# Conv's last three blocks by token half, conv's output products reordered, one query and key group normalized earlier, the first operand by single k tiles, and the last addition but one on GpSimd

## The chip, the cores and the metric

The kernel runs on one core of one Trainium2 chip. The metric is the device time of an execution in microseconds (us). Before the change the median of three executions is 1030.29 us (1028.41 to 1030.9). The engines go by their names in the profile: PE is TensorE (PEld its weight loads), DVE is VectorE, ACT is ScalarE, POOL is GpSimd, SP is SyncE, which issues most DMAs.

## The reference

Two decoder layers over 256 tokens of width 1024; the first mixes tokens by attention, the second by a convolution module. Each sublayer is normalized, scaled and shifted by vectors that come from a conditioning vector `c`, and gated.

```python
for i in range(2):
    mod = (silu(c) @ ada_w[i] + ada_b[i]).reshape(B, 3, 3, D)
    shift, scl, gate = mod[:, :, 0], mod[:, :, 1], mod[:, :, 2]
    pre = lambda z, j: rms_norm(z, norm_g[i, j]) * (1 + scl[:, j]) + shift[:, j]
    x = x + 0.5 * gate[:, 0] * swiglu_ffn(pre(x, 0), ffn_w_in[i, 0], ffn_w_out[i, 0])
    h = pre(x, 1)
    y = moba_attention(h, ...) if i == 0 else conformer_conv(h, ...)
    x = x + gate[:, 1] * y
    x = x + 0.5 * gate[:, 2] * swiglu_ffn(pre(x, 2), ffn_w_in[i, 1], ffn_w_out[i, 1])
# attention: 16 heads of 64, q and k RMS-normed per head, causal, ALiBi
# conv: u = h @ w_pw1 + b; u = a * sigmoid(g); 31-tap causal depthwise conv;
#       silu(layer_norm(u)) @ w_pw2 + b
```

## The kernel before

**Products.** Every large product is made in three: operand and weight are each split into a high part and a rest (`hh`, `hl` for the operand, `whi`, `wlo` for the weight), and PE adds hh·whi, hh·wlo and hl·whi (lines 675 to 677 in `mm3`). A weight tile of 128x1024 comes in by a DMA that SP issues (`raw`, L210); ACT makes `whi` (L250), DVE makes `wlo` (L225). Folds of the conditioning matrix run in between as chains of multiply-adds on DVE (L289, L291; L529, L531 for the first sublayer). All of this is one stream of steps: `take(n)` sets how many steps each following `block()` of products issues, so `take` and the place of the calls in the Python code set where the weight work stands in the queues of ACT and DVE. Six raw buffers and six split pairs go round.

**Order.** Nothing sorts the instructions: each engine runs its own in the order in which the code issues them, and an instruction that waits holds all behind it on its engine.

**Start.** The first operand is made by quarters `q` of the width (`early_turn`, L586 to L599). Per quarter ACT reads two k tiles from PSUM and scales them (L595, twice 128x256), copies both into `hh` in one instruction (L598, 128x512), and DVE subtracts for `hl` (L599, 128x512). Until the first product PE runs 8 idle matmuls (`IDLE_FIRST`).

**Attention.** The sublayer is an order written by hand, in which U(t, unit, u) is a block of projections, R(t, g) the sum of squares of one token half's query and key group (ACT L864, DVE L867 and L868 for `s`, and a power on POOL for `r`, L869), N(t, g) the multiplication by it (DVE L875, `z`), Q(t, g) its transposes on PE (L887) with copies on ACT, S scores (DVE L919 and ACT L925 behind them), M the division of the probabilities `p` (DVE L936), X their transposes (PE L943), V the products with the values. Its output operand is split at L966 and L967. R(1,1) comes a few calls ahead of N(1,1), with U(0,C,1) and V(0) between them.

**Convolution.** Eight blocks of 128 channels. U(b) projects a block, `glu` gates it (ACT L1096, DVE L1097), `park` and `spread` send it out and back by POOL's DMAs, `wide` makes a block's tap weights (POOL or DVE, L1050), C(b) is the depthwise convolution (64 matmuls, L1122, then ACT L1126 adds the bias into `v`), VT(b) transposes `v` to tokens by channels (PE L1136). When all eight blocks are there, `moments` and `norm` (DVE L1141 to L1152, POOL L1148) normalize a token half t, `swish(t, h)` transposes it back (PE L1159) with a Silu on ACT (L1163), `put(t, h)` makes `hh` and `hl` (DVE L1175, L1176), and O(t, j) is the output product, j over the four quarters of the contraction. `run_sums` is a group of 16 one-column matmuls (L347). `residual(t)` (DVE L609, L612) adds the result to `x`, then follows the next sublayer's normalization (POOL L631, DVE L638, PE L654, ACT and DVE L660 to L670); the callback `after()` is the one for token half 0. C(6) and C(7) run as two token halves of 128, C(0) to C(5) whole.

**End.** The last `residual` of each token half goes in pieces of 512, 256 and 256 columns; each piece is one multiplication (L609), one addition (L612), both on DVE, and one DMA to the output (L614).

## Time and profile before

| what | value |
|---|---|
| median of three executions | 1030.29 us |
| the profiled execution's own time | 1031.33 us |
| its span | 1029.6 us |
| PE busy in the span | 1013.7 us (98%) |
| DVE, ACT, POOL busy | 781.1, 488.9, 70.5 us |
| DMA moved | 256 MB, 249 GB/s |

The span is the stretch from the first instruction to the last that the profiler saw; 1.73 us of the execution's time lie around it. In order of time the span holds the first feed-forward sublayer (to about 213 us), attention (to about 340), two feed-forward sublayers (to about 722), the convolution (to about 836) and the last feed-forward sublayer. All times of instructions are us from the start of the span. "Busy" of PE counts an instruction as long as its results are on the way; matmuls overlap, and what counts for PE is the distance from one start to the next (about 0.23 us for a 128x512 product).

### The profile page before, as it was taken

Reading aid. Unit: us, or ns where it says so; the run is one execution under the profiler, and the core shown is the slowest. Engines: PE = TensorE matmul, PEld = TensorE weight load, DVE = VectorE, ACT = ScalarE, POOL = GpSimd, SP = SyncE. Lnnn points to the kernel's source line nnn. Section 1 sums busy time; section 2 is a strip of 40 time slices with the busy share of each in tenths; the row PEclk is TensorE's granted clock in tenths of the full one; section 3 lists DMA queues with packets and bytes.
Section 4 is the critical chain, followed back from the end, with each engine's and each line's share of the span. In section 5 each row is a group of like instructions: output and inputs, shape, how many; then the busy total and the mean of one; then the engine's idle time right before and its main releaser. Section 6 shows DMA issues by size and latency. Waiting matters only on the chain.

```text
span 1029.6 us, 14614 instructions
## 1 busy us (share of the span) xinstructions
PE 1013.7 (98%) x5457; PEld 821.8 (80%) x5457; DVE 781.1 (76%) x1167; ACT 488.9 (47%) x762; POOL 70.5 (7%) x123
## 2 busy tenths in 40 slices
PE   9999999999999999999999999999999999999998
PEld 6788787887776888887888887888986778888886
DVE  5789888989997788878778878786684788656633
ACT  4454344566675544444455444354522556444420
POOL 3000000002210000000010000000166000000000
PEclk9999999999999999999999999999999999999999
DMA  9989999948765399999839898886596468766611
GB/s 336 338 277 329 319 329 322 317 154 272 245 217 188 115 324 317 300 319 305 295 101 307 288 317 293 286 289 202 174 275 203 133 200 299 240 211 215 218 38 41
DMA packets 183754, 256.08 MB, mean 249 GB/s; under 512 B 9045, under 2 KB 132726, under 8 KB 183684
## 3 DMA queue, kind: packets, MB, share of 16 engines
q1 hardware_dynamic: 180928, 248.55, 72.4%
q0 software_dynamic: 2608, 6.55, 2.3%
q8 instruction: 43, 0.70, 0.3%
q14 instruction: 27, 0.22, 0.1%
q10 hardware_dynamic: 148, 0.06, 0.0%
HBM read 252.89 MB, written 2.23 MB: 248 GB/s over the span
## 4 chain that ended last, share of the span: by engine, by line
PE 82%; DVE 8%; ACT 4%; issue 3%; DMA 3%; POOL 0%; SPq 0%; POOLq 0%; DVEq 0%; ACTq 0%
PE u L677 15%; PE u L675 14%; PE u L676 14%; PE y L675 10%; PE y L677 10%; PE y L676 10%; DVE wlo L225 2%; DVE acc L291 2%; PE m L753 2%; PE m L1122 2%; ACT whi L250 1%; DMA raw<-in_conv_w_pw_dram 1%; ACT p L925 1%; DMA raw<-in_ffn_w_in_dram 1%; DMA raw<-in_attn_w_qkv_dram 1%
## 5 line engine op out<-in xcount | busy, mean ns | idle before, releaser
L225 DVE TENSOR_TENSOR wlo<-raw,whi 128x1024 fp32r<-128x1024 f32 x320 | 382.4, 1224 | 31.4 <-ACT whi L250 31.2
L250 ACT ACTIVATE whi<-raw 128x1024 fp32r<-128x1024 f32 x320 | 328.4, 1054 | 151.0 <-DMA raw<-in_ffn_w_in_dram 67.6
L675 PE MATMUL u<-whi,hh 128*128 128x512 f32 x672 | 266.4, 396 | 1.5 <-ACT hh L669 1.1
L677 PE MATMUL u<-whi,hl 128*128 128x512 f32 x672 | 262.9, 391 | 0.2
L676 PE MATMUL u<-wlo,hh 128*128 128x512 f32 x672 | 261.9, 390 | 0.3 <-DVE wlo L225 0.3
L291 DVE SCALAR_TENSOR_TENSOR acc<-raw,sc,acc 128x512 f32<-128x512 f32 x224 | 172.1, 768 | 5.0
L677 PEld LDWEIGHTS u<-whi,hl 128*128 128x128 f32 x672 | 126.1, 188 | 29.7 <-DVE hl L599 1.9
L675 PEld LDWEIGHTS u<-whi,hh 128*128 128x128 f32 x672 | 126.2, 188 | 28.1 <-ACT hh L669 1.9
L676 PEld LDWEIGHTS u<-wlo,hh 128*128 128x128 f32 x672 | 126.3, 188 | 25.6 <-DVE wlo L225 0.6
L675 PE MATMUL y<-whi,gh 128*128 128x512 f32 (+1 forms) x356 | 138.9, 390 | 0.2 <-ACT gh L761 0.2
L677 PE MATMUL y<-whi,gl 128*128 128x512 f32 (+1 forms) x356 | 137.9, 387 | 0.0
L676 PE MATMUL y<-wlo,gh 128*128 128x512 f32 (+1 forms) x356 | 137.8, 387 | 0.0
L675 PE MATMUL y<-whi,hh 128*128 128x512 f32 (+1 forms) x256 | 96.7, 378 | 1.5 <-DVE hh L1175 0.8
L762 DVE TENSOR_TENSOR gl<-m,gh 128x512 fp32r<-128x512 f32 (+1 forms) x48 | 31.0, 646 | 84.7 <-ACT gh L761 84.5
L677 PE MATMUL y<-whi,hl 128*128 128x512 f32 (+1 forms) x256 | 94.0, 367 | 0.0
L676 PE MATMUL y<-wlo,hh 128*128 128x512 f32 (+1 forms) x256 | 93.9, 367 | 0.0
L761 ACT ACTIVATE gh<-m 128x512 fp32r<-128x512 f32 (+1 forms) x48 | 27.0, 563 | 133.6 <-PE m L753 133.6
L723 ACT ACTIVATE sg<-u 128x256 f32<-128x256 f32 x84 | 32.1, 382 | 109.4 <-PE u L677 109.3
L675 PEld LDWEIGHTS y<-whi,gh 128*128 128x128 f32 x356 | 66.9, 188 | 15.5 <-issue 0.8
L677 PEld LDWEIGHTS y<-whi,gl 128*128 128x128 f32 x356 | 66.8, 188 | 14.3 <-DVE gl L762 0.4
L676 PEld LDWEIGHTS y<-wlo,gh 128*128 128x128 f32 x356 | 66.9, 188 | 13.3
L675 PEld LDWEIGHTS y<-whi,hh 128*128 128x128 f32 x256 | 48.7, 190 | 12.5 <-issue 3.5
(178 smaller groups left out, 872.7 us busy)
## 6 DMA issues: line engine op xcount, KB each, us to landing
raw<-in_ffn_w_in_dram SPq DMA_DIRECT2D x164, 512.0 KB, 5.0
raw<-in_ada_w_dram SPq DMA_DIRECT2D x144, 512.0 KB, 5.2
raw<-in_ffn_w_out_dram SPq DMA_DIRECT2D x88, 512.0 KB, 5.2
raw<-in_attn_w_qkv_dram SPq DMA_DIRECT2D x24, 512.0 KB, 5.0
raw<-in_conv_w_pw_dram SPq DMA_DIRECT2D x24, 512.0 KB, 6.3
raw<-in_ffn_w_in_dram SPq DMA_DIRECT2D x24, 256.0 KB, 4.5
R<-d POOLq DMA_DIRECT2D x32, 142.0 KB, 6.3
raw<-in_attn_w_o_dram SPq DMA_DIRECT2D x8, 512.0 KB, 4.5
```

Source lines behind the costliest of these rows:

```text
L225: (eng or nc.vector).tensor_tensor(lo, raw, hi.bitcast(F32), op=ALU.subtract)
L250: self.nc.scalar.activation(hi, self.like(self.raws[i], hi), AF.Copy)
L291: nc.vector.scalar_tensor_tensor(dst, raw[:, i, :], self.sc[:, k : k + 1], dst, op0=ALU.mult, op1=ALU.add)
L675: nc.tensor.matmul(out, lh, rh, start=start, stop=False)
L676: nc.tensor.matmul(out, lh, rl, start=False, stop=False)
L677: nc.tensor.matmul(out, ll, rh, start=False, stop=stop)
L723: nc.scalar.activation(sg, ps[:, 0:256], AF.Silu)
L753: nc.tensor.transpose(ps[:, o : o + P], g[:, t, k * P : k * P + P], self.ident)
L761: nc.scalar.activation(hi, src, AF.Copy)
L762: nc.vector.tensor_tensor(lo, src, hi.bitcast(F32), op=ALU.subtract)
L925: nc.scalar.activation(p[:, c0:c1], p[:, c0:c1], AF.Exp, bias=st[:, t : t + 1], scale=-1.0, accum_out=st[:, 2 + t : 3 + t],)
L1122: nc.tensor.matmul(ps[32 * g : 32 * g + 32, :], wd[b][:, q, g, :], R[b][:, g, 4 * q + t0 : 4 * q + t0 + n], start=q == 0, stop=q == 7,)
```

## The change

Line numbers of the changed kernel are 10 higher from `residual` on, 11 to 12 higher at the end of `conv`.

1. **First operand.** For the first quarter (q = 0) ACT copies each k tile into `hh` right behind its own scaling, and DVE subtracts each k tile by itself: two instructions of 128x256 for one of 128x512 on either engine. `IDLE_FIRST` goes from 8 to 6.
2. **Last residual.** The second and third piece share one `tmp` tile, and for token half 1 the addition of the second piece (columns 512 to 767) is issued to POOL.
3. **Attention.** N(1,1) moves ahead of U(0,C,1) and V(0).
4. **Convolution.** The five weight steps that the first block of the loop issued are spread as two in U(5) and two in U(6), with the rest later. C(5), C(6), C(7) run for token half 0 first, then for token half 1. swish(0, h) and put(0, h) stand between the second halves, `run_sums` behind them. The output products change from O(0,0) O(0,1) O(0,2) O(0,3) | residual(0) | O(1,0) O(1,1) after() O(1,2) O(1,3) to O(0,0) O(0,1) O(1,0) O(0,2) O(0,3) | residual(0) | O(1,1) O(1,2) after() O(1,3), and the takes around them change.

```diff
-IDLE_FIRST = 8
+IDLE_FIRST = 6
@@ early_turn, in the loop over the two k tiles i
-        nc.scalar.activation(hi, h, AF.Copy)
-        return lambda: nc.vector.tensor_tensor(lo, h, hi.bitcast(F32), op=ALU.subtract)
+            if not q:
+                nc.scalar.activation(hi[:, i, :], h[:, i, :], AF.Copy)
+        if q:
+            nc.scalar.activation(hi, h, AF.Copy)
+
+        def put():
+            for i in (slice(0, 1), slice(1, 2)) if not q else (slice(0, 2),):
+                nc.vector.tensor_tensor(lo[:, i, :], h[:, i, :], hi[:, i, :].bitcast(F32), op=ALU.subtract)
+
+        return put
@@ residual
-            tmp = self.two.tile([P, 512], F32, name="tmp", tag="tmp", bufs=1)[:, 0:n]
...
-            nc.vector.tensor_tensor(x[:, s], x[:, s], tmp, op=ALU.add)
+            c = slice(o % 512, o % 512 + n)
+            if c.start == 0:
+                half = self.two.tile([P, 512], F32, name="tmp", tag="tmp", bufs=1)
+            tmp = half[:, c]
+            nc.vector.scalar_tensor_tensor(tmp, y[h][:, c], f, gate[:, s], op0=ALU.mult, op1=ALU.mult)
+            eng = nc.gpsimd if t and o == 512 and last else nc.vector
+            eng.tensor_tensor(x[:, s], x[:, s], tmp, op=ALU.add)
@@ attention
-        U(0, C, 0), X(0), S(1), M(1), R(1, 1), Q(0, 1), U(0, C, 1), V(0), N(1, 1)
+        U(0, C, 0), X(0), S(1), M(1), R(1, 1), Q(0, 1), N(1, 1), U(0, C, 1), V(0)
@@ conv
         glu(4)
+        take(2)
         for b in range(4):
             if b < 3:
                 U(b + 5)
-            if b == 0:
+            if b == 1:
                 take(0)
...
-        C(5)
+        C(5, 0, P), VT(4), C(6, 0, P)
         self.step(), self.step()
-        VT(4), C(6, 0, P), VT(5), take(4), self.block(), C(7, 0, P), VT(6, (0,))
+        VT(5, (0,)), take(2), self.block(), C(7, 0, P), VT(6, (0,))
         take(0)
-        C(6, P, P), VT(7, (0,)), moments(0), norm(0, 0), norm(0, 1)
-        C(7, P, P), VT(6, (1,))
+        C(5, P, P), VT(7, (0,)), moments(0), norm(0, 0), norm(0, 1)
+        C(6, P, P), VT(5, (1,)), swish(0, 0)
+        C(7, P, P), VT(6, (1,)), put(0, 0), swish(0, 1)
+        VT(7, (1,)), moments(1), put(0, 1), norm(1, 0), norm(1, 1)
         self.run_sums(True)
-        VT(7, (1,)), swish(0, 0), moments(1), put(0, 0)
-        swish(0, 1), norm(1, 0), put(0, 1), norm(1, 1)
-        O(0, 0), swish(1, 0), O(0, 1), put(1, 0), swish(1, 1), put(1, 1), take()
-        O(0, 2), O(0, 3)
+        (the four y banks are allocated here)
+        O(0, 0), swish(1, 0), take(2), O(0, 1), put(1, 0), swish(1, 1), put(1, 1)
+        O(1, 0), O(0, 2), O(0, 3)
         self.residual(0, y[0], gate, 1.0)
-        O(1, 0), O(1, 1)
-        after()
-        O(1, 2), O(1, 3)
+        take(1), O(1, 1), O(1, 2), after(), take(0), O(1, 3)
         self.residual(1, y[1], gate, 1.0)
```

DVE in attention, around N(1,1), before the change (`s` is the sum of squares of R(1,1), `z` the product of N(1,1), `acc` a fold of the conditioning matrix, `wlo` a weight rest):

```order
L868 TENSOR_SCALAR s_2452<-s_2452 128x8
L291 SCALAR_TENSOR_TENSOR acc<-raw,sc,acc 128x512 x2
L225 TENSOR_TENSOR wlo<-raw,whi 128x1024
L875 TENSOR_TENSOR z<-y,r_2453 128x512
L225 TENSOR_TENSOR wlo<-raw,whi 128x1024
L291 SCALAR_TENSOR_TENSOR acc<-raw,sc,acc 128x512 x2
```

and with the change:

```order
L878 TENSOR_SCALAR s_2452<-s_2452 128x8
L885 TENSOR_TENSOR z<-y,r_2453 128x512
L291 SCALAR_TENSOR_TENSOR acc<-raw,sc,acc 128x512 x2
L225 TENSOR_TENSOR wlo<-raw,whi 128x1024 x2
L291 SCALAR_TENSOR_TENSOR acc<-raw,sc,acc 128x512 x2
```

Two folds and one weight rest that stood between `s` and `z` now stand behind `z`; `r`, which `z` reads, is made from `s` on POOL.

ACT in the convolution's loop, before the change (`whi` is a weight's high part, `sg` the sigmoid of a block, `v` a block's result with its bias):

```order
L250 ACTIVATE whi<-raw 128x8x128
L1096 ACTIVATE sg<-u,cols 128x256
L250 ACTIVATE whi<-raw 128x8x128 x3
L250 ACTIVATE whi<-raw 128x1024 x2
L1096 ACTIVATE sg<-u,cols 128x256
L1126 ACTIVATE v<-m,cols 128x256
```

and with the change:

```order
L250 ACTIVATE whi<-raw 128x8x128
L1106 ACTIVATE sg<-u,cols 128x256
L250 ACTIVATE whi<-raw 128x8x128 x2
L1106 ACTIVATE sg<-u,cols 128x256
L1136 ACTIVATE v<-m,cols 128x256
L250 ACTIVATE whi<-raw 128x8x128
L250 ACTIVATE whi<-raw 128x1024
L1106 ACTIVATE sg<-u,cols 128x256
```

The first `v`, and the `sg` ahead of it, stand behind two weights' high parts in place of five.

DVE at the end of the program, before the change (token half 1's last residual):

```order
L609 SCALAR_TENSOR_TENSOR tmp<-y,gate 128x512
L612 TENSOR_TENSOR x_118<-x_118,tmp 128x512
L609 SCALAR_TENSOR_TENSOR tmp<-y,gate 128x256
L612 TENSOR_TENSOR x_118<-x_118,tmp 128x256
L609 SCALAR_TENSOR_TENSOR tmp<-y,gate 128x256
L612 TENSOR_TENSOR x_118<-x_118,tmp 128x256
```

and with the change:

```order
L620 SCALAR_TENSOR_TENSOR tmp<-y,gate 128x512
L622 TENSOR_TENSOR x_118<-x_118,tmp 128x512
L620 SCALAR_TENSOR_TENSOR tmp<-y,gate 128x256 x2
L622 TENSOR_TENSOR x_118<-x_118,tmp 128x256
```

One of the two additions of 128x256 has left DVE; it is POOL's last instruction now, and SP's order of output DMAs is as it was.

## Rows read from the trace of the kernel before

**Rows 1.** The page's parts 1 and 4: busy per engine, the chain's shares.

```profile
PE 1013.7 (98%) x5457; PEld 821.8 (80%) x5457; DVE 781.1 (76%) x1167; ACT 488.9 (47%) x762; POOL 70.5 (7%) x123
PE 82%; DVE 8%; ACT 4%; issue 3%; DMA 3%; POOL 0%; SPq 0%; POOLq 0%; DVEq 0%; ACTq 0%
```

**Rows 2.** Timeline 13:25: start, duration, instruction, [idle before <- releaser].

```profile
15.96 0.63 ACT L598 ACTIVATE hh<-hf 128x512 fp32r<-128x512 f32 x1
...
17.37 0.50 PE L677 MATMUL u<-whi,hl 128*128 128x512 f32 x1
...
20.23 3.61 DVE L531 SCALAR_TENSOR_TENSOR acc<-raw,sc,acc 128x256 f32<-128x256 f32 x7
...
24.18 0.60 PE L543 MATMUL m<-one,acc 128*128 128x1 f32 x4
```

**Rows 3.** Timeline 262:268, around N(1,1) and Q(1,1) of attention.

```profile
263.17 1.53 DVE L291 SCALAR_TENSOR_TENSOR acc<-raw,sc,acc 128x512 f32<-128x512 f32 x2
263.40 2.00 POOL L869 TENSOR_TENSOR r<-s,mhalf 128x8 f32<-128x8 f32 x1 [8.90 <-DVE s L868]
...
265.75 0.68 DVE L875 TENSOR_TENSOR z<-y,r 128x512 f32<-128x512 f32 x1
266.35 1.21 DVE L225 TENSOR_TENSOR wlo<-raw,whi 128x1024 fp32r<-128x1024 f32 x1
...
266.58 0.63 PE L887 MATMUL m<-ident,z 128*128 128x128 f32 x4 [1.46 <-DVE z L875]
```

**Rows 4.** Attention's rest: window, POOL, DVE, PE; window's columns: span, PE, PEld, DVE, ACT, POOL.

```profile
267.00:306.00 39.00, 38.53 (x214) 28.29 (x212) 36.47 (x95) 26.62 (x71) 6.65 (x4) 1.00 0.70 232
...
277.06 1.64 POOL L869 TENSOR_TENSOR r<-s,mhalf 128x8 f32<-128x8 f32 x1 [5.36 <-DVE st L934]
...
277.62 1.14 PE L943 MATMUL m<-ident,p 128*128 128x128 f32 x6
...
293.78 0.69 DVE L867 TENSOR_REDUCE s<-sq 128x8 f32<-128x512 f32 x1 [1.01 <-ACT sq L864]
...
306.39 0.50 PE L675 MATMUL y<-whi,hh 128*128 128x512 f32 x1 [0.71 <-ACT hh L966]
```

**Rows 5.** Timeline 762:812, PE and ACT in the convolution.

```profile
773.45 1.06 ACT L250 ACTIVATE whi<-raw 128x1024 fp32r<-128x1024 f32 x1 [2.01 <-DMA raw<-in_conv_w_pw_dram]
...
775.29 0.44 PE L1136 MATMUL y<-ident,v 128*128 128x128 f32 x2 [1.34 <-ACT v L1126]
...
793.27 3.66 PE L1122 MATMUL m<-R,wd 128*32 128x256 f32 x64
...
799.49 1.95 PE L1122 MATMUL m<-R,wd 128*32 128x128 f32 x64
...
809.77 0.74 PE L675 MATMUL y<-whi,hh 128*128 128x512 f32 x1 [0.79 <-DVE hh L1175]
```

**Rows 6.** Windows 810:812 and 812:814; columns as in Rows 4, then PEclk, DMA share, GB/s.

```profile
810.00:812.00 2.00, 2.00 (x5) 1.54 (x6) 1.93 (x6) 1.48 (x5) 0.00 (x0) 0.50 0.04 14
812.00:814.00 2.00, 2.00 (x8) 1.57 (x7) 1.60 (x4) 0.00 (x0) 0.00 (x0) 0.68 0.00 0
```

**Rows 7.** Timeline 835:850, start of the last feed-forward sublayer.

```profile
839.22 0.68 DVE L609 SCALAR_TENSOR_TENSOR tmp<-y,gate 128x512 f32<-128x512 f32 x1
...
844.36 1.10 PE L654 MATMUL m<-ident,z 128*128 128x128 f32 x8 [0.70 <-DVE z L638]
...
849.29 0.50 PE L675 MATMUL u<-whi,hh 128*128 128x512 f32 x1 [1.09 <-ACT hh L669]
```

**Rows 8.** Groups of POOL; timelines of DVE in 761:767, of DVE and SP at the end.

```profile
L1050 POOL TENSOR_TENSOR wd<-w,mask 128x1024 f32<-128x1024 f32 x6 | 11.5, 1924 | 0.1
...
761.49 5.32 DVE L225 TENSOR_TENSOR wlo<-raw,whi 128x1024 fp32r<-128x1024 f32 x3
...
1025.93 1.25 SPq L614 DMA_DIRECT2D out_dram<-x  x2
...
1026.39 0.42 DVE L612 TENSOR_TENSOR x<-x,tmp 128x256 f32<-128x256 f32 x1
```

More of the change, by code (lines that the diff above doesn't have):

```diff
@@ L607, in residual @@
             s, h = slice(o, o + n), o // 512
-            tmp = self.two.tile([P, 512], F32, name="tmp", tag="tmp", bufs=1)[:, 0:n]
-            nc.vector.scalar_tensor_tensor(
-                tmp, y[h][:, o % 512 : o % 512 + n], f, gate[:, s], op0=ALU.mult, op1=ALU.mult
-            )
-            nc.vector.tensor_tensor(x[:, s], x[:, s], tmp, op=ALU.add)
+            c = slice(o % 512, o % 512 + n)
[5 more added lines that the diff above has]
+            eng.tensor_tensor(x[:, s], x[:, s], tmp, op=ALU.add)
             if last:
@@ L1240, in conv @@
         VT(3), wide(7, nc.vector)
-        C(5)
+        C(5, 0, P), VT(4), C(6, 0, P)
         self.step(), self.step()
-        VT(4), C(6, 0, P), VT(5), take(4), self.block(), C(7, 0, P), VT(6, (0,))
+        VT(5, (0,)), take(2), self.block(), C(7, 0, P), VT(6, (0,))
         take(0)
-        C(6, P, P), VT(7, (0,)), moments(0), norm(0, 0), norm(0, 1)
-        C(7, P, P), VT(6, (1,))
+        C(5, P, P), VT(7, (0,)), moments(0), norm(0, 0), norm(0, 1)
+        C(6, P, P), VT(5, (1,)), swish(0, 0)
+        C(7, P, P), VT(6, (1,)), put(0, 0), swish(0, 1)
+        VT(7, (1,)), moments(1), put(0, 1), norm(1, 0), norm(1, 1)
         self.run_sums(True)
-        VT(7, (1,)), swish(0, 0), moments(1), put(0, 0)
-        swish(0, 1), norm(1, 0), put(0, 1), norm(1, 1)
-        O(0, 0), swish(1, 0), O(0, 1), put(1, 0), swish(1, 1), put(1, 1), take()
-        O(0, 2), O(0, 3)
+        for h in range(2):
+            for t in range(2):
+                y.setdefault(t, []).append(self.bank("y"))
+        O(0, 0), swish(1, 0), take(2), O(0, 1), put(1, 0), swish(1, 1), put(1, 1)
+        O(1, 0), O(0, 2), O(0, 3)
         self.residual(0, y[0], gate, 1.0)
-        O(1, 0), O(1, 1)
-        after()
-        O(1, 2), O(1, 3)
+        take(1), O(1, 1), O(1, 2), after(), take(0), O(1, 3)
         self.residual(1, y[1], gate, 1.0)
```

## The prediction

> **What bounds the kernel now.** I read the page's busy shares and its chain of waits first. PE is busy 98% of the span and holds 82% of the chain; DVE holds 8%, ACT 4% [rows 1]. So the time is PE's work plus the few stretches in which PE waits, and a change that leaves PE's products alone can only move those. I went through PE's timeline for its waits and looked in each place at what the releasing engine had been doing. The change touches four: the first operand (14 to 25 us), attention between 262 and 306, the convolution with what follows it (762 to 850), and the last 5 us. The rest I take as carried along: PE is late or early by the same amount until something else ends last.
>
> **First operand: -0.2.** The first product that needs `hl` starts at 17.37, right behind a subtraction that begins when the whole `hh` is there (15.96 plus 0.63) [rows 2]. By k tiles the copy ends about half of 0.63 earlier and the subtraction is half as long, but DVE is still busy with a weight rest at that time; by hand this product starts 0.69 earlier. The gain doesn't last: the first `m` from a fold, at 24.18, needs DVE's fold of the conditioning matrix, which ends at 20.23 + 3.61 = 23.84 [rows 2]. The fold itself stands behind the weight rests and these behind ACT, whose extra copy costs it about 0.1. So 24.18 becomes some 23.95. From there on DVE sets the pace of the next quarters. I take -0.2, bounds 0 and -0.69. The two idle products fewer cost nothing: they fill a time in which PE has no operand.
>
> **Attention: +1.9.** Before, DVE goes from `s` at 263.17 to two folds (1.53) and a weight rest, then `z` at 265.75, and the next weight rest starts at 266.35. POOL makes `r` from `s` beside it, from 263.40 for 2.00. PE stands still for 1.46 before the transposes of `z` at 266.58 [rows 3]. With `z` ahead, PE's wait gets shorter, but DVE now waits for POOL with nothing to do, and everything that it did meanwhile comes after. The power on POOL takes 1.64 where DVE doesn't run folds beside it [rows 4], so `z` starts at 263.40 + 1.64 + 0.05 = 265.09, which is 0.66 earlier for PE. Then come `z` (0.60 from its start to the next: 266.35 - 265.75) and the three moved instructions (265.75 - 263.17 = 2.58): the next weight rest starts at 265.09 + 0.60 + 2.58 = 268.27 in place of 266.35. DVE is 1.92 late; with 2.00 for the power it would be 2.28.
>
> Does that come back? Between 267 and 306 DVE is busy 36.47 of 39 us [rows 4]. The longest of its few idle times is 1.01 at 293.78, for ACT's squares, and ACT there works on scores that DVE gave it. So that idle time moves along. PE takes its probabilities from DVE just in time: the six transposes at 277.62 last 1.14, and the second head's are held inside [rows 4]. I find no slack there: PE arrives 0.66 early and leaves 1.9 late. The next wait, 0.71 at 306.39 for ACT's `hh` [rows 4], hangs on the same chain of DVE and ACT. I take +1.9; the bounds are +2.3 (2.00 for the power), and -0.66, if DVE catches up somewhere and only PE's earlier transposes count.
>
> **Convolution and what follows: -2.2, or -0.5.** Five terms.
>
> (a) Loop. PE waits 1.34 at 775.29 for `v`, because ACT's add of the bias stands behind five high parts, the last of which got its data only at 773.45 [rows 5]. With two high parts ahead of it, `v` is ready before PE asks. I take -1.35 at this place, bound 0 if the next `v`, which still stands behind two high parts with late data, takes its place.
>
> (b) C(5) in two halves: a whole block takes 3.66 for 64 products, a half 1.95 for 64 [rows 5], so 2 x 1.95 - 3.66 = +0.24. More weights are loaded for the same columns.
>
> (c) The way to the first output product. Before, PE waits 0.79 for `hh` of DVE and starts at 809.77 [rows 5]. Now the normalization and the Silu of token half 0 run beside C(6) and C(7) of half 1, and `hh` is there when PE comes. But three waits are new, by hand: VT(7) for a `v` that stands behind four high parts of about 1.06 on ACT (some 0.4), the first transposes back for the normalization (some 0.6), and PE's 16 tiny matmuls lie where nothing else can. With (a) and (b), I get O(0,0) at about 808.95, 0.8 earlier than before.
>
> (d) The clock. [...] Before the fall PE had run 16 one-column matmuls and a few transposes and then stood still, some 3.7 us of little work. With the change I count about 2.7 us of it by hand; in attention, where PE stood for 1.46 [rows 3], the granted clock was 1.00 behind it [rows 4]. So I think it more likely (6 in 10) that the clock stays up. [...]
>
> (e) The output products and the start of the next sublayer. O(1,0) now comes early, and needs `put(1, 0)`, which on DVE stands behind a weight rest that waits for ACT; some 0.9 of waiting. residual(0) starts about 1.5 later than before, since four weight rests of 1.21 are ahead of it, and token half 0's transposes and operand then wait some 0.75 and 1.2. With these, the gains of (c) and (d) are used up when the next sublayer's first product starts (835.3 in both). But token half 1's residual starts at 836.25 by my count, before at 839.22 behind three weight rests; it is 3 us earlier, and PE's waits of 0.70 at 844.36 and 1.09 at 849.29 [rows 7], with the transposes that they hold apart, go. The product at 849.29 then starts at 847.05.
>
> Sum: -2.2 if the clock stays up, -0.5 with the fall (1.64 of loss, all of it behind O(0,0)). Bounds: all of it gone, 1.34 + 0.79 + 1.64 + 0.70 + 1.09 - 0.24 = -5.3, and, with the fall and new waits as long as the old ones, +0.5.
>
> **The end: 0.** DVE's last addition starts at 1026.39 for 0.42, and SP issues its two DMAs from 1025.93 in 1.25 together, the second right behind that addition [rows 8]. DVE now does one addition less: 0.46 earlier. POOL's addition has no row. A product of 128x1024 takes POOL 1.92 [rows 8], DVE's subtraction of that size takes 1.21 [rows 3]; by that ratio, 1.59, the 0.42 become about 0.67, from about 1025.6 to 1026.3. SP issues in its order, so the second DMA goes out 0.33 behind POOL's end, at about 1026.6: -0.2. Against it stand the three weight rests that ran beside such a POOL product: 5.32 in place of 3 x 1.21 [rows 8], 1.7 longer. DVE's last addition runs beside POOL's; if held to POOL's end it is where it was before. I take 0, bounds -0.46 and +1.2. [...]
>
> **Sum.** -0.2 + 1.9 - 2.2 + 0 = -0.5 with the clock up; -0.2 + 1.9 - 0.5 = +1.2 with the fall. The profiled execution took 1031.33, so 1030.8 or 1032.5; it lay 1.04 above the median of 1030.29, so in the median's frame 1029.8 or 1031.5.
>
> **Rivals.**
> 1. *The clock falls all the same*: 1031.5. For it: PE still has a stretch of tiny matmuls and waits before O(0,0). Against it: the stretch is a quarter shorter.
> 2. *The moved normalization costs nothing*: DVE has slack that I don't see, and PE keeps its 0.66: -0.2 - 0.66 - 2.2 = -3.1, so 1027.2, or 1028.9 with the fall. For it: DVE is idle 2.5 us between 267 and 306, and PE is busy 38.53 of 39 us there [rows 4], so only little is held now. Against it: the places where PE waits are those that DVE feeds last.
> 3. *The convolution gains more*: the waits that I count as new in (c) and (e) are mine by hand; if they are half as long, some 2 us more go: about 1027.8.
> 4. *Slower: DVE becomes the bound in attention and the output products give the rest away.* The wait for POOL costs 2.3, the clock falls, and O(1,0) waits for `put(1, 0)` behind the weight rest, so that residual(1) isn't early. Then the convolution is worth +0.5 and the end +0.5: +3.1 to +3.5, 1033.6. It decides from about 2 us of wait at O(1,0), which is two weight rests in place of one.
> 5. *The edits do nothing that lasts*: PE's later waits take each gain and each loss back. 1030.3.
>
> **How the numbers follow.** Forecast 0.32, rival 1 0.22, rival 2 0.18, rival 3 0.10, rival 4 0.11, rival 5 0.07. A measurement of this kernel tells about 0.3% from no change, 3.1 us: faster is below 1027.2, slower above 1033.4. Faster gets half of rival 2, which lies on the bound, a third of rival 3 and the bounds of the forecast's convolution term (to -5.3): 0.09 + 0.04 + 0.11 = 0.24. Slower gets most of rival 4, and a little of rival 1: 0.10. Within: 0.66. The range that leaves out 1 in 10 on either side goes from 1026.3 to 1033.3.
>
> **What would show it.** Forecast right in attention: DVE idle about 1.8 before `z` of N(1,1), `z` at about 265.1, and a PE wait of some 1.5 to 2.5 at the transposes of probabilities near 278. It is wrong if that wait isn't there. Convolution: no wait at the first VT, PEclk at 1.00 behind O(0,0), a wait before O(1,0), no waits of PE at token half 1's start of the last sublayer. The end: POOL's addition at 0.5 to 0.9, and the last DVE addition not longer than 0.6. The forecast as a whole is wrong if PE's waits between 306 and 748, which I left as they are, change by more than 1 us.

## The result, and the profile after

The changed kernel takes 1037.01 us (median of five executions, 1034.06 to 1039.12) against 1029.94 of the kernel before on the same occasion (five executions): the ratio is 1.0062, 95% interval 1.0045 to 1.0079. That is 6.4 us slower by the ratio, where 0.5 us faster was forecast and 1033.3 was the end of the range.

The profiled execution has a span of 1035.23 us, 5.7 more than the 1029.55 before (the two executions took 1037.01 and 1031.33). PE's busy time is the same within 2 us (1013.7 before, [rows 1]), so again it is waits that count.

The page's part 1 of the changed kernel:

```profile
PE 1015.4 (98%) x5519; PEld 824.4 (80%) x5519; DVE 785.1 (76%) x1167; ACT 489.9 (47%) x764; POOL 70.9 (7%) x124
```

I compared when PE starts the same product in both traces. The difference, after less before, in us:

| point of the program (time before) | after less before | added in this stretch | forecast |
|---|---|---|---|
| second product group of the last quarter of the first operand (51) | +1.17 | +1.17 | -0.2 |
| first output product of attention (306) | +2.93 | +1.76 | +1.9 |
| first convolution transposes, L1136 (775) | +0.93 | -2.0 | -1.35 |
| first output product of the convolution (810) | +2.99 | +2.06 | -0.8 in all to here |
| last feed-forward sublayer, in full run (859) | +3.28 | +0.29 | -0.5 in all, with the clock's fall |
| PE's last product | +3.30 | 0 | |
| end of the span | +5.7 | +2.4 | 0 |

Four stretches, then: the start, attention, the convolution (+0.35 in all between 306 and 859) and the end. Here are the rows of each.

**Start.** Timeline of the changed kernel, ACT and PE, answering to [rows 2] (columns: start, duration, instruction, idle time before and its releaser):

```profile
24.10 0.58 PE L543 MATMUL m<-one,acc 128*128 128x1 f32 x4 [0.67 <-DVE acc L531]
...
25.63 1.06 ACT L250 ACTIVATE whi<-raw 128x1024 fp32r<-128x1024 f32 x1 [1.19 <-DMA raw<-in_ffn_w_in_dram]
26.60 1.00 ACT L595 ACTIVATE hf<-m,mod,mod 128x256 f32<-128x256 f32 x2
```

The product at 24.18 before is at 24.10 here, waiting for DVE's fold: PE's lead of 0.8 at 17 us is gone, as forecast. But then ACT waits 1.19 for a weight's data, and the next quarter's operand (`hf`) is queued behind it. In the kernel before, ACT went through the same place without a wait:

```profile
24.02 1.99 ACT L250 ACTIVATE whi<-raw 128x1024 fp32r<-128x1024 f32 x2
25.92 1.01 ACT L595 ACTIVATE hf<-m,mod,mod 128x256 f32<-128x256 f32 x2
```

**Attention.** DVE, POOL and PE of the changed kernel around N(1,1), answering to [rows 3], and the next places where PE waits, answering to [rows 4]:

```profile
264.10 0.17 DVE L878 TENSOR_SCALAR s<-s 128x8 f32<-128x8 f32 x1
266.08 0.69 DVE L885 TENSOR_TENSOR z<-y,r 128x512 f32<-128x512 f32 x1 [1.81 <-POOL r L879]
266.69 1.53 DVE L291 SCALAR_TENSOR_TENSOR acc<-raw,sc,acc 128x512 f32<-128x512 f32 x2
```
```profile
264.41 1.64 POOL L879 TENSOR_TENSOR r<-s,mhalf 128x8 f32<-128x8 f32 x1 [8.90 <-DVE s L878]
```
```profile
266.92 0.63 PE L897 MATMUL m<-ident,z 128*128 128x128 f32 x4 [0.78 <-DVE z L885]
...
275.50 0.63 PE L897 MATMUL m<-ident,z 128*128 128x128 f32 x4 [0.58 <-DVE z L885]
...
280.41 1.27 PE L953 MATMUL m<-ident,p 128*128 128x128 f32 x6 [1.54 <-DVE p L946]
...
309.32 0.50 PE L685 MATMUL y<-whi,hh 128*128 128x512 f32 x1 [0.21 <-ACT hh L976]
```

DVE stands still for 1.81 in front of `z`, and PE pays at the transposes of the probabilities (1.54).

**Convolution.** PE's waits of the changed kernel from 794 us to the last sublayer, answering to [rows 5] and [rows 7], and the granted clock behind the first output product (windows; columns as in [rows 6]), answering to [rows 6]:

```profile
799.88 1.96 PE L1132 MATMUL m<-R,wd 128*32 128x128 f32 x64 [1.07 <-DMA R<-d]
...
807.04 0.63 PE L1169 MATMUL m<-ident,z 128*128 128x128 f32 x4 [0.66 <-DVE z L1162]
...
811.84 1.05 PE L347 MATMUL m<-one,acc 128*128 128x1 f32 x8 [0.69 <-ACT hf L1173]
...
821.86 0.50 PE L685 MATMUL y<-whi,hh 128*128 128x512 f32 x1 [0.85 <-DVE hh L1185]
...
836.14 0.66 PE L664 MATMUL m<-ident,z 128*128 128x128 f32 x4 [0.37 <-DVE z L648]
...
840.75 0.50 PE L685 MATMUL u<-whi,hh 128*128 128x512 f32 x1 [0.75 <-ACT hh L679]
```
```profile
814.00:816.00 2.00, 2.00 (x7) 1.56 (x6) 1.57 (x4) 0.00 (x0) 0.00 (x0) 0.55 0.00 0
816.00:818.00 2.00, 2.00 (x9) 1.66 (x8) 0.00 (x0) 0.10 (x1) 0.00 (x0) 0.59 0.57 169
```

The wait of 1.34 at the first transposes is gone, and so are the 0.79 at the first output product and the two of token half 1 at 844 and 849 (0.70 and 1.09); together they were 3.92. Six others stand in their place, 4.39 together, and the granted clock fell again (0.55 and 0.59 in these windows, 0.50 and 0.68 before [rows 6]).

**The end.** Timeline of the changed kernel's last 7 us, answering to [rows 8], and the closing instructions of POOL's and SP's sequencers in the changed kernel (view of one source line; columns: shortest, median and longest duration in ns, start of the first and of the last):

```profile
1026.89 3.55 SPq L624 DMA_DIRECT2D out_dram<-x  x3
...
1028.32 0.76 DVE L620 SCALAR_TENSOR_TENSOR tmp<-y,gate 128x256 f32<-128x256 f32 x2 [1.45 <-PE y L687]
1028.88 0.72 POOL L622 TENSOR_TENSOR x<-x,tmp 128x256 f32<-128x256 f32 x1 [182.38 <-DVE tmp L620]
1029.11 0.78 DVE L622 TENSOR_TENSOR x<-x,tmp 128x256 f32<-128x256 f32 x1
```
```profile
L1320 POOLq EVENT_SEMAPHORE  x4: 17/17/17, 1034.5 to 1035.1; - x4
L1320 POOLq DRAIN  x3: 46/102/5582, 1028.9 to 1035.0; - x3
L1320 SPq DRAIN  x3: 7/7/7, 1032.0 to 1034.7; - x3
```

The same line in the kernel before, where it is L1308:

```profile
L1308 POOLq EVENT_SEMAPHORE  x4: 17/17/17, 1028.8 to 1029.4; - x4
L1308 POOLq DRAIN  x3: 46/102/5417, 843.2 to 1029.3; - x3
L1308 SPq DRAIN  x3: 7/7/7, 1028.7 to 1029.0; - x3
```

POOL ends its program with a drain. In the kernel before it starts at 843.2, when POOL has its last power in hand, lasts 5.42 us and is over at 848.6, 180 us before anyone asks for it. In the changed kernel it starts at 1028.9 with the addition and lasts 5.58, to 1034.4. SP has seen the last output land and is through at 1032.0; the engines' last meeting, which POOL opens with a semaphore, begins at 1034.5, right behind POOL's drain (in the kernel before at 1028.8, right behind SP's). The last output itself lands 3.80 behind the start of PE's last product, 3.81 before: the way of the data costs nothing. In both, the drain ends 4.83 behind the end of POOL's last operation (843.23 + 0.55 and 1028.88 + 0.72).

### The profile page after: what moved, and what is told of

It is laid out like the page before. It is cut to its first block, busy times and chain, and to the rows that moved or that the text cites. A ratio compares the mean times of both kernels' runs of the same rounds, so it can differ in the third digit from the quotient of the medians.

```text
span 1035.2 us, 14738 instructions
## 1 busy us (share of the span) xinstructions
PE 1015.4 (98%) x5519; PEld 824.4 (80%) x5519; DVE 785.1 (76%) x1167; ACT 489.9 (47%) x764; POOL 70.9 (7%) x124
```

## The experiments

A ratio is that to the kernel before on the same chip, with its 95% interval; one thousandth is 1.03 us. From the traces I give the lead or lag of PE against the profiled execution of the kernel before, at the same points as above (+ is later).

**Each part alone.** The first four kernels are the kernel before with one part of the change each.

```diff
# e1_end
+            eng = nc.gpsimd if t and o == 512 and last else nc.vector
+            eng.tensor_tensor(x[:, s], x[:, s], tmp, op=ALU.add)
# e2_attention
-R(1, 1), Q(0, 1), U(0, C, 1), V(0), N(1, 1)
+R(1, 1), Q(0, 1), N(1, 1), U(0, C, 1), V(0)
# e3_start
-IDLE_FIRST = 8
+IDLE_FIRST = 6
...
+            if not q:
+                nc.scalar.activation(hi[:, i, :], h[:, i, :], AF.Copy)
...
+            for i in (slice(0, 1), slice(1, 2)) if not q else (slice(0, 2),):
# e4_conv
+        take(2)
...
-        C(5)
+        C(5, 0, P), VT(4), C(6, 0, P)
...
-        O(1, 0), O(1, 1)
-        after()
-        O(1, 2), O(1, 3)
+        take(1), O(1, 1), O(1, 2), after(), take(0), O(1, 3)
```

> The kernel before with part 2 alone: the addition of columns 512 to 767 of token half 1 on POOL. Theory (closing drain): POOL's last instruction of the program is a drain that ends 4.83 us after the end of POOL's last addition; in the kernel before it lies at 843 to 849 us and is hidden, here it holds the end: the output's last DMA lands as before, the span ends 2.2 to 2.4 us later, ratio about 1.0022. Rival (the sum on record): the addition's own length and the sharing with DVE set the end, 0 us, bounds -0.5 and +1.2, and the drain costs nothing.

Measured: 1.0033 (1.0020 to 1.0045). In its trace the last pieces run as in the changed kernel:

```profile
1023.27 0.76 DVE L612 SCALAR_TENSOR_TENSOR tmp<-y,gate 128x256 f32<-128x256 f32 x2 [1.45 <-PE y L679]
1023.84 0.72 POOL L614 TENSOR_TENSOR x<-x,tmp 128x256 f32<-128x256 f32 x1 [181.82 <-DVE tmp L612]
```

In the kernel before, the first of these multiplications is here:

```profile
1025.02 0.42 DVE L609 SCALAR_TENSOR_TENSOR tmp<-y,gate 128x256 f32<-128x256 f32 x1 [1.45 <-PE y L677]
```

From 1023.27 to the span's end at 1030.18 are 6.91 us; before they are 4.53 (from 1025.02 to 1029.55). So the end costs 2.4, as the drain has it (1034.4 less 1032.0 in the changed kernel), and PE's part of this execution happened to be 1.7 shorter than in the profiled one of before. The time, 3.4 us longer with an interval from 2.1 to 4.6, holds 2.4.

> The kernel before with part 3 alone: N(1,1) ahead of U(0,C,1) and V(0). Theory (DVE waits for POOL and is the bound until 306): z at about 265.1, DVE idle 1.8 before it, PE waits 1.5 to 2 at the transposes of probabilities near 278, first product of the output projection 1.8 to 2.0 later than 306.39, span +1.8. Rival (the loss of 1.8 in the whole change came from the clock that falls near 282, with which PE's wait there ends): without the first part's shift the clock may stay up, and the span is then +0.3 at most. A clock that falls and still leaves the 306 product at +1.8 speaks for the first.

Measured: 1.0014 (0.9998 to 1.0030). The interval reaches no change, so it is the trace that tells. In it PE's lag goes from +0.20 at 51 us to +2.05 at 306 and stays (+1.72 at the end):

```profile
265.19 0.69 DVE L875 TENSOR_TENSOR z<-y,r 128x512 f32<-128x512 f32 x1 [1.81 <-POOL r L869]
```
```profile
266.03 0.63 PE L887 MATMUL m<-ident,z 128*128 128x128 f32 x4 [0.75 <-DVE z L875]
...
274.61 0.63 PE L887 MATMUL m<-ident,z 128*128 128x128 f32 x4 [0.60 <-DVE z L875]
...
279.53 1.27 PE L943 MATMUL m<-ident,p 128*128 128x128 f32 x6 [1.53 <-DVE p L936]
...
308.44 0.50 PE L675 MATMUL y<-whi,hh 128*128 128x512 f32 x1 [0.71 <-ACT hh L966]
```

DVE's row first, then PE's waits: the same 1.81 and the same places as in the changed kernel. The clock stayed at 1.00 in this trace, while in the changed kernel's it fell near 282; the lag at 306 is the same. So the clock's fall there cost nothing that lasted, and DVE's wait is the cause.

> The kernel before with part 1 alone: first operand by single k tiles, six idle products. Theory (a fetch of instructions lies on one DMA engine in front of a weight): PE starts 0.8 earlier, so the fetch at 23.5 to 24 comes 0.5 earlier and delays another weight, the one that ACT needs next; by 28 us the gain is gone, +0.4, and again at 51 us, +1.2 in all; span +1.0 to +1.3. Rival (the sum on record): the gain shrinks to -0.2 at 24.2 and stays. Second rival (chance of one execution): the shift differs from run to run and its median is near 0.

Measured: 1.0012 (1.0000 to 1.0024). In the trace +0.63 at 28 us, +0.70 at 51, +0.99 at the end: neither the first rival's gain that stays nor the theory's +1.2 at 51. The second rival, chance, comes up again below.

> The kernel before with part 4 alone. Theory from the two traces: the spread weight steps bring the blocks 3.6 us forward by 797 us, the halves and the output products give it all back by 836 (a wait for spread data near 800, one for the normalization near 807, the clock that falls at the first output product as before), and PE is 0.2 to 0.5 late at 859 us: span 0 to +0.5. Rival (the sum on record): -2.2 with the clock up, -0.5 with the fall.

Measured: 1.0004 (0.9994 to 1.0014). The clock stayed up in its trace, unlike in the trace of before; PE goes from +0.51 at 306 to -0.85 at 859, a gain of 1.36. By my estimate from the windows of [rows 6], in which 0.50 and 0.32 of the clock are missing for 2 us each, 1.64 of it is the clock: +0.3 at the same clock, as in the changed kernel (+0.35, both with the fall). PE's waits are those of the changed kernel, 1.05 for the spread data, 0.67, 0.63 and 0.85. The -2.2 that was forecast for the clock up is not there.

The four losses add up: 3.3 + 1.4 + 1.2 + 0.4 = 6.3 thousandths, with 6.2 measured for the whole change. Each has an interval of 1.0 to 1.6 thousandths on either side, so the sum shows no hindrance between the parts and doesn't exclude a small one.

**Whether the drain is the cause at the end.** If POOL's drain is what costs, it is the place of POOL's last operation that counts, and neither its length nor what it does.

```diff
# e7_end_half0
-            eng = nc.gpsimd if t and o == 512 and last else nc.vector
+            eng = nc.gpsimd if not t and o == 512 and last else nc.vector
# e13_probe, e15_probe_early: the kernel before, and behind the output's last DMA
# of token half 1 (e13) or of token half 0 (e15):
+                    probe = self.tiny.tile([P, 1], F32, name="probe", tag="probe")
+                    nc.gpsimd.tensor_tensor(probe, tmp[:, 0:1], self.mhalf[:, 0:1], op=ALU.mult)
# e16_end_back: the changed kernel with nc.vector for that addition
```

> The kernel before with POOL's addition in token half 0's last residual in place of token half 1's, some 10 us earlier. Theory (closing drain): the drain of 4.83 us behind POOL's addition ends before the output's last DMA has landed; the end is as before, span 0, within 0.2, in the trace from PE's last product on. Rival (the loss of 2.3 us is POOL's slow addition and the sharing with DVE): half 0's output comes later by as much, but half 1's end as before too, so the time is also 0; what tells the two apart is the first run of part 2, where the last DMA landed as early as before and the span still ended 2.3 later.

Measured: 0.9997 (0.9984 to 1.0010). The drain begins at 1013.8 and lasts 5.59, so it is over at 1019.4, and POOL is ready when it is wanted at 1026.7:

```profile
L1310 POOLq EVENT_SEMAPHORE  x4: 17/17/17, 1026.7 to 1027.3; - x4
L1310 POOLq DRAIN  x3: 46/102/5593, 1013.8 to 1027.2; - x3
```

The same addition on POOL, 10 us earlier, costs nothing that time or trace shows: from the end of PE's last product to the end of the span it takes 4.45 (4.57 before, 6.95 in the changed kernel).

> The kernel before with one tiny product more on POOL (128x1, result used by nobody), which waits for DVE's last multiplication of the program; nothing else in the output's way is changed. Theory (closing drain): POOL's drain ends about 4.83 us behind that product, at about 1031.6 in the time of before, where POOL is wanted at 1028.8: +2.5 to +2.9 from PE's last product to the end. Rival (POOL's addition cost by its length and by sharing with DVE): 0, within 0.2.

Measured: 1.0061 (1.0049 to 1.0074). In its trace the drain lasts 5.30 from 1030.2, to 1035.5, while SP is through at 1032.5:

```profile
L1311 POOLq DRAIN  x3: 46/102/5299, 1030.2 to 1036.0; - x3
L1311 SPq DRAIN  x3: 7/7/7, 1032.5 to 1035.7; - x3
```

That is 2.9 at the end, as expected, against 2.4 for the addition of 128x256: the product of 128x1 comes later (its drain begins at 1030.2 with PE 3.75 late, the addition's at 1028.9 with PE 3.30 late). But the timed loss was 6.3, and PE was 3.75 late in the trace before the end was reached.

> The tiny product on POOL again, now behind token half 0's last multiplication, some 8 us earlier; all else as in the kernel with the tiny product at the end. Theory (the closing drain is all that it costs): the drain ends before POOL is wanted, ratio 1.000, within 0.001. Rival (the tiny product's own tile or the instruction costs the rest of the program something, which would explain that its timed loss of 6 us was above the 2.9 of the end in its trace): ratio 1.002 to 1.004 here too.

Measured: 1.0036 (1.0022 to 1.0050). The rival holds: with the tiny product where its drain is hidden, 3.7 us are lost all the same, though its drain is over at 1024.1, before SP is through at 1030.9:

```profile
L1311 POOLq DRAIN  x3: 46/102/5295, 1018.8 to 1031.5; - x3
L1311 SPq DRAIN  x3: 7/7/7, 1030.9 to 1031.2; - x3
```

The difference between the two kernels, 1.0061 and 1.0036, is 2.6 us, which fits the drain's 2.9 in the trace. What the probe's tile or instruction costs elsewhere isn't settled: both traces have PE 1.7 late at 51 us and a wait of 2.5 and 3.1 at the first transposes of the convolution, where the kernel before has 1.34 [rows 5]; the convolution's weights take 7.1 and 7.4 us from issue to landing at the median there, 5.8 to 6.3 in the traces without the probe. Whether the additional tile moves others in memory, and whether that is the cause, wasn't tried.

> The changed kernel with the addition back on DVE, nothing else. Theory (closing drain): PE's last product to the end takes 4.5 to 4.6 as in the kernel before, not 6.9; of the loss of 6.4 us 2.3 to 3.4 go, ratio 1.003 to 1.004; between this and the kernel with both repairs (1.0020) lies attention's share, 1.4 to 2. Rival (attention's share was small, most of the loss is the end): ratio near 1.002 here too.

Measured: 1.0031 (1.0020 to 1.0043), so half of the loss is the end's. In the trace the end of PE's last product is 4.44 from the end of the span, near the theory's 4.5 to 4.6.

**Whether DVE's wait for POOL is the cause in attention.** `z` early, but its `r` ready:

```diff
# e6_r_early (the kernel before)
-U(0, C, 0), X(0), S(1), M(1), R(1, 1), Q(0, 1), U(0, C, 1), V(0), N(1, 1)
+U(0, C, 0), R(1, 1), X(0), S(1), M(1), Q(0, 1), N(1, 1), U(0, C, 1), V(0)
# e12_mended: the changed kernel, with this R(1, 1) and the addition back on DVE
```

> The kernel before with N(1,1) ahead of U(0,C,1) as in part 3, and R(1,1) moved up too, to right behind U(0,C,0), so that POOL's power runs while DVE does S(1) and M(1). Theory (part 3 loses because DVE stands still for POOL): no idle time of DVE before z, PE's wait of 1.46 at the transposes of z gone, the transposes of probabilities near 278 not later than before, output projection's first product 0 to 1 us earlier, span 0 to -1. Rival (part 3 loses because two folds and a weight rest come later than z, whatever DVE does meanwhile): still +1.5 to +2 near 278 and at the end.

Measured: 1.0005 (0.9990 to 1.0020), no difference that this tells. In the trace `z` follows `p` with no wait, folds and weight rest come behind it as in the change, and PE is 0.20 early at 306:

```profile
262.48 0.55 DVE L936 TENSOR_SCALAR p<-p,st 128x128 f32<-128x128 f32 x2
262.94 0.69 DVE L875 TENSOR_TENSOR z<-y,r 128x512 f32<-128x512 f32 x1
263.55 1.53 DVE L291 SCALAR_TENSOR_TENSOR acc<-raw,sc,acc 128x512 f32<-128x512 f32 x2
```
```profile
277.28 1.27 PE L943 MATMUL m<-ident,p 128*128 128x128 f32 x6 [0.78 <-DVE p L936]
```

So the three instructions behind `z` cost nothing by themselves; the idle time does. PE's lead of 1.3 at the transposes of `z` is given back at the probabilities (0.78), which hang on DVE's sum of work.

> The changed kernel with two repairs: the addition back on DVE, and R(1,1) moved up to right behind U(0,C,0). Theory (the loss of 6.4 is 2.3 to 3.4 of the closing drain, 1.4 to 1.9 of DVE's wait in attention, and the rest in the start and the convolution): ratio 1.000 to 1.002, a span 4 to 5 us shorter than that of the changed kernel. Rival (the parts hinder one another beyond their sum): still over 1.003.

Measured: 1.0020 (1.0011 to 1.0028). The two repairs take 4.2 of the 6.4 us. Against 1.0031 with the end alone repaired, attention's share in the changed kernel is about 1.1 us in time; the traces say 1.76 to 1.85 between 51 and 306 us (changed kernel, e2_attention, e16_end_back), and the intervals hold both. In this kernel's trace PE is 0.1 earlier at 306 than at 51: the lag of attention is gone. What is left, 2.1 us, is not assigned; parts 1 and 4 alone took 1.2 and 0.4.

**What holds the start back.**

```diff
# e9_start_idle10: part 1 with
-IDLE_FIRST = 6
+IDLE_FIRST = 10
```

> The kernel before with part 1, but ten idle products in place of six: PE's first product is held back by about 0.6 us, to near the time of before. Theory (PE's early start moves the fetch of instructions in front of the fourth weight): the fetch comes near 23.6 again, the fourth weight's last share within 1 us of its first, and at 28 us PE stands within 0.2 of before, span 0, so later idle products give a shorter time than six. Rival (ACT's extra copy and DVE's split subtraction cost it): +0.4 to +0.6 at 28 us all the same.

Measured: 0.9998 (0.9983 to 1.0012), and in the trace +1.01 at 28 us. The time is below that of six idle products, but the intervals overlap, and the trace says that my theory falls. A fetch of 16 KB of instructions (the page has 43 such packets with 0.70 MB) does lie on one DMA engine about there, one packet of 0.96 us (the window 23.5 to 24 us of before, 23 to 23.5 of the changed kernel; the columns are packets, MB and the share of 16 engines' time, in which a packet counts whole where it starts):

```profile
q8 instruction: 1, 0.02, 12.0%
```

But it starts at 23.6 in before, without a lag, and at 23.6 and 23.7 in e16_end_back and here, with lags of 0.49 and 1.01. And in every trace with a lag the same weight's data are late, as in this one, where ACT waits 1.56:

```profile
26.26 1.06 ACT L250 ACTIVATE whi<-raw 128x1024 fp32r<-128x1024 f32 x1 [1.56 <-DMA raw<-in_ffn_w_in_dram]
```

But the lag comes without part 1 too. At 28 us the kernels that leave the start alone stood at -0.13, -0.12, -0.11, +0.01, +0.30, +0.42, +0.83, +0.83 and +0.94 (the two with the probe at +1.48 and +1.59), those with part 1 at +0.38, +0.49, +0.63, +0.91 and +1.01. So the profiled execution of before was among the lucky ones. At 51 us the ten executions with the old start (before included, without the two with the probe) lie 0.37 behind it in the mean and the five with part 1 lie 0.90 behind it, so about half of the +1.17 in the table above is chance. Why the weight's data are late in some executions is open. What part 1 costs by itself (0.5 in these means, 0 to 2.4 us in the time of e3_start) isn't settled; a gain isn't there.

**What the convolution's parts give.**

```diff
# e5_loop: the kernel before with
         glu(4)
+        take(2)
         for b in range(4):
...
-            if b == 0:
+            if b == 1:
                 take(0)
# e11_idle_conv: the kernel before with, ahead of O(0, 0)
+        junk = self.bank("u")
+        for _ in range(4):
+            nc.tensor.matmul(junk, self.ones, self.ones.unsqueeze(1).to_broadcast([P, 4, P]), start=True, stop=True)
# e14_best: e6_r_early with these idle products; e17_three: that and e5_loop
```

> The kernel before with the loop's part of part 4 alone: the five weight steps of the first block spread as two and two, the three last blocks, the output products and the takes behind them as before. Theory (in the whole change the spread steps brought the blocks some 3.6 us forward by 797 us and the halves and the new order gave that back): the first output product comes 2 to 3.5 us earlier than before, the span -1.5 to -3 at the same clock, ratio 0.997 to 0.9985. Rival (the weight steps taken out of the loop come back in the tail, where ACT and DVE are as full, or the early blocks wait for the spread data): the lead is gone by the first output product, span within 0.5.

Measured: 1.0004 (0.9991 to 1.0018). The rival holds. PE is 1.43 early at the first output product, and 0.27 at 859: a weight step that left the loop comes back ahead of the output products, which wait for its rest:

```profile
820.15 0.50 PE L676 MATMUL y<-wlo,hh 128*128 128x512 f32 x1 [0.59 <-DVE wlo L225]
...
821.29 0.50 PE L676 MATMUL y<-wlo,hh 128*128 128x512 f32 x1 [0.17 <-DVE wlo L225]
```

> The kernel before with four idle products of 128x512 (0.23 us each) between the transposes back and O(0,0), where PE waits 0.8 to 0.95 for hh. Theory (the clock falls behind the stretch of tiny matmuls and standing still, in most executions): PE is fed through its wait, the granted clock stays at 1.00 from 810 to 814, span -1.6 against an execution with the fall, and the median -1 to -1.5. Rival (what counts is the tiny matmuls and waits before that, 806 to 809): the clock falls as before, span 0 to +0.2.

Measured: 0.9998 (0.9984 to 1.0011). In the trace the idle products start at 809.04 and O(0,0) is not later for them; the clock stays at 1.00, and PE gains 1.5 between 810 and 814:

```profile
810.00:812.00 2.00, 2.00 (x9) 1.54 (x9) 1.93 (x6) 1.80 (x6) 0.21 (x1) 1.00 0.06 19
812.00:814.00 2.00, 2.00 (x12) 1.65 (x11) 1.88 (x5) 0.35 (x1) 0.00 (x0) 1.00 0.00 0
```

The median does not show it, though its interval doesn't exclude the theory's 1 to 1.5 us either. Of the fourteen traces without idle products ten have the fall behind the first output product; of the three with them (this one and the next two) none has. So the fall isn't in every execution without them either, and what the idle products save in the mean is, as an estimate from the 1.5 gained here against a fall, not above 1.5.

> The kernel before with R(1,1) and N(1,1) moved up together and with the four idle products ahead of O(0,0). Theory: -0.3 of attention and -1 to -1.5 of the clock, ratio 0.9985 to 0.999. Rival (the clock falls all the same): -0.3 to 0.

Measured: 0.9996 (0.9986 to 1.0005). The clock stayed up, against the rival, but the time doesn't tell the theory's 0.9985 to 0.999 from no change.

> The kernel before with three edits that look good in the traces: R(1,1) and N(1,1) moved up together, the weight steps of the convolution's loop spread, four idle products ahead of O(0,0). Theory: the spread steps take away the wait at the first VT, which is 0.4 to 3.3 in the executions so far, and the lead lasts now that the clock stays up; ratio 0.997 to 0.999. Rival (the lead is given back at the weight rests of the output products, as with the spread steps alone): 0.9995 to 1.0005.

Measured: 0.9998 (0.9988 to 1.0007), the rival: the first transposes no longer wait, and the two waits for weight rests stand at 818.68 (0.59) and 819.81 (0.17) as with the loop alone. Both kernels beat the changed one by more than 6 us (ratios 0.9996 and 0.9998 against 1.0062); neither is told from the kernel before.

## Why the prediction was wrong

- **The step that failed: the end, "0, bounds -0.46 and +1.2".** It measured +2.4 in the trace and, by the part alone, 3.4 (2.1 to 4.6) in time, the largest single loss. For the way of the data the 0 was right: POOL's addition took 0.72 (0.67 by the ratio of rows 8 to rows 3), and the last output DMA was issued 0.08 earlier against PE's last product than before and landed as early. (One sign failed there: DVE's last addition beside it took 0.78, where not more than 0.6 was said.) But I took the landing of that DMA for the end. In these traces the engines' last meeting begins only when POOL's drain is over, however early the output has landed (at 1034.5 behind a drain to 1034.4 in the changed kernel, at 1029.4 behind one to 1029.4 in e1_end, at 1035.5 behind one to 1035.5 in e13_probe, with SP through at 1032.0, 1027.0 and 1032.5), and this drain ends 4.83 us behind its last operation. The row was in the trace of before, at 843.2, hidden because POOL had nothing to do for the last 180 us; busy times don't count a drain, and I had read only those. The addition took 1.7 times as long on POOL as on DVE before (0.72 against 0.42), but the price lay elsewhere.
- **Attention, "+1.9", was right**, with its mechanism: forecast and measured (in e2_attention) are `z` at 265.09 and at 265.19, an idle time of DVE of 1.8 and of 1.81, the transposes of the probabilities 1.9 later than 277.62 and at 279.53, behind a wait of 1.5 to 2.5 and of 1.53, and +1.76 to +1.85 at the output projection. Rival 2 is out. e6_r_early shows that the idle time, not the new order, is the cause. In time the loss is about 1.1 to 1.4 and, taken alone, not told from nothing.
- **The convolution, "-2.2, or -0.5", was mis-sized by about 0.8** in both cases: +0.35 with the clock's fall, and -1.36 in e4_conv with the clock up against a before with the fall. (a) was right: the wait is gone in all six traces with the weight steps spread. The -2.0 there is partly chance; between 720 us and the first transposes nine executions with the old loop lie 0.5 ahead of the profiled one of before in the mean (from 1.5 ahead to 0.75 behind), the six with the new one 1.8 ahead, so the gain is 1.3, as forecast. (d) went as in rival 1: the clock fell in the profiled execution; over the kernels it falls in ten of fourteen traces, so 6 in 10 for a clock that stays up looks too high. The 1.64 that the forecast puts on the fall is shown by no run; it was my estimate from the granted clock of 0.50 and 0.68 between 810 and 814 [rows 6], and what the runs showed in its place is 1.54 from the first output product to 859 us (e1_end and e7_end_half0, with the clock up, against before) and 1.5 between 810 and 814 (e11_idle_conv against before). What failed is (c): the first output product came not 0.8 earlier but as late as before. I had counted the wait for the normalization (0.66 measured, 0.6 forecast) but not that C(7) for half 0 now comes before the second halves and asks for its spread data 1.07 too early, nor the wait of 0.69 inside the tiny matmuls. (e) was half right: the waits of token half 1 are gone, O(1,0) waits 0.85 (0.9 forecast), but the next sublayer's first product came 2.4 later than before, where no more than the 1.64 of the fall was forecast (0.7 in e4_conv with the clock up, where 0 was forecast), so that half 1's gain only paid that back. One pair of traces is little here: between 720 and 859 us seven executions with the old convolution lie from 3.1 ahead of the profiled one of before to 0.6 behind it (0.7 ahead in the mean), the four with the new one 0.2 ahead in the mean. That is a loss of 0.5, and 1.0004 in time.
- **The start, "-0.2", is not told from what was measured**: +1.2 (0 to 2.4) in time with part 1 alone, +0.5 to +1.2 at 51 us in the five traces with it, of which about 0.4 is the luck of the profiled execution of before. The forecast that the lead is lost at 24 us was right; that PE then falls behind by a weight's late data was not in it.
- **The sum.** -0.2, +1.9, -2.2 (-0.5 with the fall), 0 were forecast; +1.17, +1.76, +0.35, +2.4 is what the two traces show, 5.7 in all. Against the forecast's +1.2 with the fall that is 4.5 too much: 2.4 from the end, 1.4 from the start, 0.85 from the convolution. The range left out the time because two terms had no room on the bad side: the end stopped at +1.2 and the start at 0. With every term at its bad bound the sum is only +4.0 (0 + 2.3 + 0.5 + 1.2). Rival 4 named the slower side, with attention at 2.3 and the convolution at +0.5, but not the engine that set the end.

## What to carry to other kernels

Before work is given to an engine that has been idle for the last part of a program, look at how the program closes: its last instructions (drains, semaphores) are in the trace though no busy time counts them. Here a drain of 5.4 us that had been hidden came to light when POOL got late work, and cost 2.4; the same addition 10 us earlier was free. On an engine that is busy throughout, as DVE is here (36.47 of 39 us [rows 4]), look whether a result that is moved forward finds its input ready: in e2_attention PE's wait for `z` fell from 1.46 [rows 3] to 0.75, DVE stood idle for POOL instead, and that idle time was paid in full (1.81 of it, 1.85 of lag). With the producer moved forward as well it was gone (e6_r_early). And compare traces over more than one execution of unchanged code: here the start, the first transposes of the convolution and the clock behind 810 us each differed by 1 to 2 us from one execution to the next, and two executions with the same convolution code by up to 3.6 us over the stretch from 720 to 859.

## What the runs showed of the hardware

- POOL's closing drain begins about with POOL's last operation and lasted 5.42 us where that is a power of 128x1 (before, e16_end_back), 5.58 and 5.59 where it is an addition of 128x256 (changed kernel, e1_end; e7_end_half0), 5.30 where it is a product of 128x1 (e13_probe, e15_probe_early). It ended 4.83 behind the end of the power (0.55) in before and of the addition (0.72) in the changed kernel.
- An addition of 128x256 took POOL 0.72 (changed kernel, e1_end) and DVE 0.42 (before); DVE's addition that ran beside POOL's took 0.78 (changed kernel, e1_end).
- The granted clock fell to 0.50 in attention of the changed kernel too (0.50 from 282 to 284, 0.71 to 286), behind a wait of PE of 1.54 and short transposes; in e2_attention, behind a wait of 1.53 at the same place, it stayed at 1.00. The same code gets it or not: with the old output products' code unchanged the clock fell about the first of them in before, e2_attention, e3_start, e6_r_early and e9_start_idle10 and stayed up in e1_end and e7_end_half0, and from that product to 859 us the two took 1.54 us less than before.
